# A hybrid decoder step on one NeuronCore: a tile of its own for retrieved values, and transposes of repeated keys one step later

## The chip, the cores and the metric

The kernel runs on one core of one Trainium2 chip. The time is the device time of one execution in microseconds (us), and the median of several executions is compared. The engines of the core are TensorE (PE, matrix multiplication, with PEld for the loading of its stationary operand), VectorE (DVE), ScalarE (ACT), GpSimd (POOL) and SyncE (SP, which here only issues transfers). Each engine works through its own instructions in order; semaphores hold it until what it needs is there.

## What is computed

One step of a decoder layer for 256 prompt tokens and 8 × 8 sample tokens, 320 columns in all. `trunk` runs a SwiGLU block, a token mixer and a second SwiGLU block. The mixer's one input projection feeds an mLSTM branch with 4 heads of 256 × 256 state and a dilated attention branch with 8 heads; sigmoid gates merge the two. The sample tokens start from a given state `C0`, `n0` of each of 8 sequences and read a cache of 2048 keys and values. The part of the reference that the change touches is the mLSTM of one chunk:

```python
num = jnp.einsum('bhts,bshv->bthv', wgt, v) \
    + jnp.transpose(sc, (0, 2, 1))[..., None] * jnp.einsum('bthk,bhkv->bthv', q, C0)
den = jnp.sum(wgt, axis=-1) + sc * jnp.einsum('bthk,bhk->bht', q, n0)
h = num / jnp.transpose(jnp.maximum(jnp.abs(den), jnp.exp(-m)), (0, 2, 1))[..., None]
...
C_new = sT[..., None, None] * C0 + jnp.einsum('bhs,bshk,bshv->bhkv', e, k, v)
n_new = sT[..., None] * n0 + jnp.einsum('bhs,bshk->bhk', e, k)
```

For the sample tokens, `q · C0` is what the kernel calls retrieval, and `C_new` is the state update, for 8 sequences × 4 heads.

## The kernel before, in words

**The weight stream.** All weights are float32 and come through one stream. A job is 256 output columns; a chunk is four k-tiles of 128 × 256 of a job (512 KB). SP loads a chunk into one of 5 `raw` buffers, ACT casts it to the upper part `hi` (L225) and DVE subtracts for the lower part `lo` (L226), each with 3 buffers. PE then makes three matmuls for every 128 × 128 block (`hi` by the upper part of x, `hi` by its lower part, `lo` by the upper), 24 for a chunk, into a PSUM tile `fg`. These are the instructions called `fg` in the profile, written by the helper at L144.

**Everything else** is written as Python generators, and `run_job` (from L272) sets the order: before the matmuls of chunk `ci` it splits chunk `ci + 2` if that isn't done, runs one step of the generators in `even` or in `odd` alternately, by a pace of 8 in 15 one step of `slow`, and one of each in `every`, then issues loads ahead up to chunk `ci + 7`. So what a step issues stands in each engine's queue between the work of two chunks. `mlstm` (L979) is in `odd`, one step every two chunks, 48 `fg` matmuls apart; the attention of the sample tokens is in `slow`. The small matmuls and transposes (L337) of these go to `bg`, a PSUM tag with 4 slots.

**SP** issues all transfers in the order written. A load into a tile waits, on SP, until the tile that had its slot is no longer in use, and a transfer waits for the one issued eight before.

**The tile pool `m2`** (`m2_tile`, L500): 9 slots of 128 × 512 that go round in order of allocation. Each request takes the slot whose last holder is oldest, and the first instruction that writes the new tile waits until the last reader of the old one is done, be it an engine or a transfer. The states `C` (two for each pair of sequences, loaded by `load_c`, updated in place at L1135 and written back to `out_C_sample`), `vq`, `z`, `krep`, `vs`, `kw`, `kr`, `cn` and `isb` all live there.

**One head of the mLSTM**, step by step. `prep(h)`: decay terms `z` (DVE, ACT), `krep`, the sample keys repeated for 4 sequences (POOL, L1046), and `vs`, a cast of the sample values (ACT, L1057). `front(h)`: q · k products, transposes of `k` to `ka` and of `krep` to `kb` on PE, then on ACT `kw` from `ka` (L1089) and `kr` from `kb` (L1090). `update(h)`: PE multiplies `vh` by `kw` into the new prompt state, ACT copies it to `cn` (L1102), and POOL and ACT make `qm` (L1022) and the first `ks` (L1031 to L1033) from `kr`; then the next two states are loaded (`load_cc`). Then eight steps, two for each `s4`: `retrieve` multiplies `qm` by the states on PE, and in the last, `s4 == 3`, ACT copies the result to `isb` (L1126); `state` multiplies `ks` by `vs` and DVE adds the product to `C`; `make_ks` and `make_qm` prepare the next. `numer(h)` reads `isb`, and in the same step `prep(h + 1)` follows.

**The softmax of the sample attention** keeps small rows in `sm`, [128, 9, 32], of which each helper row is written once.

Of the kernel before, what the change touches and what calls it, by code (L numbers as in the profile page):

```python
# [9 lines left out]
F32 = mybir.dt.float32  # L10
F32R = mybir.dt.float32r
AF = mybir.ActivationFunctionType
OP = mybir.AluOpType
AX = mybir.AxisListType
# [114 lines left out]
def decoder_kernel(tc, I, O, K):  # L129
    nc = tc.nc  # L130
    V, S, G, T = nc.vector, nc.scalar, nc.gpsimd, nc.tensor
# [14 lines left out]
    def bcast(ap, n, at=1):  # L146
        shape = list(ap.shape)
        shape.insert(at, n)
        idx = [slice(None)] * len(ap.shape)
        idx.insert(at, None)  # L150
        return ap[tuple(idx)].to_broadcast(shape)
# [6 lines left out]
    def later(fn, n=1):  # L158
        later_q.append([n, fn])
# [94 lines left out]
    def bg_tile():  # L254
        return pp.tile([128, 512], F32, tag="bg", bufs=4, name="bg")
# [79 lines left out]
    def tr(out, in_):  # L335
        k = in_.shape[0]
        T.transpose(out, in_, ident[:k, :k])  # L337
# [156 lines left out]
    def mxt(shape, tag, bufs, name, dt=F32):  # L494
        return M["p"].tile(shape, dt, tag=tag, bufs=bufs, name=name)
# [4 lines left out]
    def m2_tile(name):  # L500
        return mxt([128, 512], "m2", 9, name)
# [113 lines left out]
    def sample_attention():  # L615
# [1 line left out]
        bdm = M["mix"][:, M_BD:M_BD + 32]  # L617
        kd = mxt([128, 10, 512], "kd", 1, "kd")
        pts = mxt([128, 3, 152], "pts", 1, "pts")
        sm = mxt([128, 9, 32], "sm", 1, "sm")  # L620
        G.memset(pts, 0.0)
        G.memset(sm, 0.0)
        G.memset(sm[:, 5], 1.0)
        kraw = {}

        def load_k(u, pr):
# [78 lines left out]
        def soft(u, sp):  # L705
            hg, b = divmod(u, 8)
            s = mxt([128, SCOLS], "s", 1, "ss")
            tb = ttab[:, hg]
            V.tensor_tensor(s[:, 0:128].rearrange("p (y c) -> p y c", c=4), sp[:, 0:128].rearrange("p (c y) -> p y c", c=4),
                            tb[:, 0:128].rearrange("p (y c) -> p y c", c=4), op=OP.add)  # L710
            V.tensor_tensor(s[:, 128:320].rearrange("p (x a r) -> p x a r", x=4, a=6),
                            sp[:, 128:320].rearrange("p (a x r) -> p x a r", x=4, a=6),
                            tb[:, 128:320].rearrange("p (x a r) -> p x a r", x=4, a=6), op=OP.add)
            V.tensor_tensor(s[:, 320:328], sp[:, 320:328], tb[:, 320:328], op=OP.add)
            V.tensor_reduce(sm[:, 0, 0:1], s, op=OP.max, axis=AX.X)
            V.transpose(sm[:, 1], sm[:, 0])
            V.tensor_reduce(sm[:, 2, 0:8], sm[:, 1].rearrange("p (i t) -> p t i", i=4), op=OP.max, axis=AX.X)
            V.tensor_scalar(sm[:, 3].rearrange("p (i t) -> p i t", i=4), bcast(sm[:, 2, 0:8], 4), -1.0, None, op0=OP.mult)
            V.transpose(sm[:, 4], sm[:, 3])
            S.activation(s, s, AF.Exp, bias=sm[:, 4, 0:1], accum_out=sm[:, 5, 0:1])  # L720
            return s

        def keys(u, p0, p1):
# [23 lines left out]
        def probs(s):  # L747
            pt = bg_tile()
            tr(pt[:, 0:128], s[:, 0:128])
            tr(pt[0:104, 128:256], s[:, 128:232])  # L750
            tr(pt[0:104, 256:384], s[:, 224:328])
            S.copy(pts[:, 0, 0:128], pt[:, 0:128])
            S.copy(pts[0:104, 1:3, 0:128], pt[0:104, 128:384].rearrange("p (c n) -> p c n", c=2))
            V.transpose(sm[:, 6], sm[:, 5])
            V.tensor_reduce(sm[:, 7, 0:8], sm[:, 6].rearrange("p (i t) -> p t i", i=4), op=OP.add, axis=AX.X)
            V.reciprocal(sm[:, 7, 0:8], sm[:, 7, 0:8])
            V.transpose(sm[:, 8], sm[:, 7])

        qbd = make_qbd(0)
        for u in range(17):  # L760
            yield
            if u:
                ob = bg_tile()
                pv(u - 1, ob)
            if u < 16:
                sp = scores(u, qbd)
            if u:
                if u % 4 == 1:
                    o4 = mxt([128, 4, 128], "o", 1, "osb")
                S.activation(o4[:, (u - 1) % 4], ob[:, 0:128], AF.Copy, scale=sm[:, 8, 0:1])  # L770
                if u % 4 == 0:
                    spawn(combine((u - 1) // 8, (u // 4 - 1) % 2, o4), even, True)
            if u == 16:
                break
            s = soft(u, sp)
            values(u, 4, 0, 2)
            keys(u + 1, 0, 1)
            yield
            if u < 15:
                qbd = make_qbd(u + 1)  # L780
            keys(u + 1, 1, 3)
            values(u, 1, 3, 5)
            yield
            probs(s)
            keys(u + 1, 3, 4)
            if u == 6:
                q4 = make_q4(1)
            yield
            keys(u + 1, 4, 5)
            yield  # L790
# [188 lines left out]
    def mlstm():  # L979
# [6 lines left out]
        aeT, sTb, nP, nS = M["aeT"], M["sTb"], M["nP"], M["nS"]  # L986
# [4 lines left out]
        H = {}  # L991
# [72 lines left out]

        def front(h):
            d = H[h]
            q, k, z, kp, vq, vs_ = (d[x] for x in ("q", "k", "z", "kp", "vq", "vs"))
            sp = bg_tile()
            for kt in range(2):
                mm(sp[:, 0:256], k[:, kt, 0:128], q[:, kt, 0:256], kt == 0, kt == 1)  # L1070
            for kt in range(2):
                mm(sp[:, 256:384], k[:, kt, 128:256], q[:, kt, 128:256], kt == 0, kt == 1)
            for kt in range(2):
                mm(sp[:, 384:448], k[:, kt, 192:320], q[:, kt, 256:320], kt == 0, kt == 1)
            ka, kb = bg_tile(), bg_tile()
            for j in range(2):
                for kt in range(2):
                    tr(ka[:, j * 256 + kt * 128:j * 256 + (kt + 1) * 128], k[:, kt, j * 128:(j + 1) * 128])
            for g in range(2):
                for kt in range(2):  # L1080
                    tr(kb[:, g * 256 + kt * 128:g * 256 + (kt + 1) * 128],
                       kp[:, kt * 256 + g * 128:kt * 256 + (g + 1) * 128])
            V.tensor_tensor(z[:, 0:448], z[:, 0:448], sp[:, 0:448], op=OP.mult)
            for x in (32, 96):
                V.tensor_tensor(vs_[x:x + 32], vq[x:x + 32], vs_[x:x + 32].bitcast(F32), op=OP.subtract)
            kw = m2_tile("kw").rearrange("p (j c) -> p j c", j=2)
            kr = m2_tile("kr")
            for j in range(2):
                S.activation(kw[:, j], ka[:, j * 256:(j + 1) * 256], AF.Copy, scale=aeT[:, j, 4 + h:5 + h])  # L1089
            S.copy(kr, kb)  # L1090
            d.update(kw=kw, kr=kr)

        def update(h):
            d = H[h]
            kw, ke, v = (d[x] for x in ("kw", "ke", "v"))
            cu = [bg_tile(), bg_tile()]
            for kt in range(2):
                for j in range(2):
                    mm(cu[kt][:, 0:257], kw[:, j, kt * 128:(kt + 1) * 128], v[:, j], j == 0, j == 1)
            cn = m2_tile("cn")  # L1100
            for kt in range(2):
                S.copy(cn[:, kt * 256:(kt + 1) * 256], cu[kt][:, 0:256])  # L1102
                V.tensor_copy(nP[:, 2 * h + kt:2 * h + kt + 1], cu[kt][:, 256:257])
            nk = mxt([128, 2, 8], "nk", 1, "nk")
            V.tensor_reduce(nk, ke.rearrange("p k (b t) -> p k b t", b=8), op=OP.add, axis=AX.X)
            for kt in range(2):
                V.tensor_tensor(nSv[:, :, h, kt], n0v[:, :, h, kt], sTv[:, h], op=OP.mult)
                V.tensor_tensor(nSv[:, :, h, kt], nSv[:, :, h, kt], nk[:, kt], op=OP.add)
            make_qm(h, 0)
            make_ks(h, 0)  # L1110
            later(lambda: dma(O["C_prompt"][0, 0, h].rearrange("(k p) v -> p k v", p=128),
                              cn.rearrange("p (k v) -> p k v", k=2)), 2)

        def retrieve(h, s4):
            d = H[h]
            if s4 == 0:
                d["ip"] = bg_tile()
            ip, qm = d["ip"], d["qm"]
            for kt in range(2):
                for n in range(2):  # L1120
                    x = 32 * (kt * 2 + n)
                    mm(ip[x:x + 32, 0:256], qm[:, kt, n], Cq[0][n][:, kt * 256:(kt + 1) * 256], s4 == 0, s4 == 3,
                       tile_position=(0, x))
            if s4 == 3:
                d["isb"] = m2_tile("isb")[:, 0:256]
                S.copy(d["isb"], ip[:, 0:256])  # L1126

        def state(h, b):
# [533 lines left out]
    sp = token_sums([(Y["sq"], 1)])  # L1662
# [57 lines left out]
```

## Time and profile before

| | |
|---|---|
| median of 3 runs | 2978.39 us (2976.34 to 2979.70) |
| the profiled execution | 2980.88 us |
| its span | 2979.1 us |
| mean granted PE clock | 0.992 |
| PE busy | 2923.1 us, 98% of the span |
| DVE busy | 1638.5 us, 55% |
| ACT busy | 1086.4 us, 36% |
| POOL busy | 233.8 us, 8% |
| HBM traffic | 186 GB/s over the span, up to 310 in a fortieth of it |

In a timeline the number on the left of a row is the time from the start of the span. The mixer runs from about 1060 to 1790 us, its four mLSTM heads between 1260 and 1750 us. In rows of a timeline, the bracket says how long the engine had been idle and which instruction or transfer ended the wait. A wait for several things at once is put down to the one that came last in the profile, so the name can be that of a neighbour.

### The profile page before, as it was taken

How to read it: one execution, taken by the hardware profiler on the slowest of the kernel's cores; microseconds unless marked ns; L12 is line 12 of the kernel's file. 1: busy time of each engine (PE TensorE's matmuls, PEld its weight loads, DVE VectorE, ACT ScalarE, POOL GpSimd, SP SyncE). 2: the span in 40 equal slices, each digit the busy share in tenths (PEclk: the TensorE clock that was granted, in tenths of full speed). 3: DMA queues.
4: the chain of work that ended last, by engine and by line, in shares of the span. 5: the costliest groups of instructions: out<-in, count | busy, mean ns of one | idle time of the engine just before them, and what ended most of it. 6: DMA issues, size and time to landing. Idle time of an engine off the chain costs nothing.

```text
span 2979.1 us, 51248 instructions
## 1 busy us (share of the span) xinstructions
PE 2923.1 (98%) x21522; PEld 2877.3 (97%) x21522; DVE 1638.5 (55%) x1863; ACT 1086.4 (36%) x1364; POOL 233.8 (8%) x258
## 2 busy tenths in 40 slices
PE   9999999999999999988989999999999999999998
PEld 9999999999999999987988999999999999999998
DVE  6444444444446656876877876655444444444444
ACT  5332333333335333333443433334333332333334
POOL 0000000000000000122322210000000000000000
PEclk9999999999999999999999999999999999999999
DMA  6445454444546679898989987554444444445443
GB/s 209 147 147 169 143 154 149 149 146 152 156 142 188 202 214 296 257 282 250 303 249 310 288 264 252 183 177 153 149 153 151 149 146 152 150 141 161 150 140 108
DMA packets 507763, 557.22 MB, mean 187 GB/s; under 512 B 30156, under 2 KB 452604, under 8 KB 507508
## 3 DMA queue, kind: packets, MB, share of 16 engines
q1 hardware_dynamic: 506828, 552.43, 61.0%
q8 instruction: 168, 2.75, 0.4%
q10 hardware_dynamic: 704, 1.52, 0.1%
q14 instruction: 63, 0.52, 0.1%
HBM read 521.58 MB, written 32.28 MB: 186 GB/s over the span
## 4 chain that ended last, share of the span: by engine, by line
PE 51%; issue 2%; DVE 1%; POOL 0%; DMA 0%; SPq 0%; ACT 0%; POOLq 0%; DVEq 0%
PE fg L144 48%; PE bg L144 3%; PE bg L337 0%; DVE sg L970 0%; SPq L141 0%; DVE lo L226 0%; DMA vt<-in_cache_v_dram 0%; DVE pre L940 0%; POOLq L1716 0%; DMA kraw<-in_cache_k_dram 0%; POOL Y L1680 0%; POOL ks L1033 0%; DVE C L1135 0%; DVE kd L639 0%; ACT xn L1431 0%
## 5 line engine op out<-in xcount | busy, mean ns | idle before, releaser
L226 DVE TENSOR_TENSOR lo<-raw,hi 128x1024 fp32r<-128x1024 f32 (+1 forms) x780 | 961.0, 1234 | 973.5 <-ACT hi L225 955.1
L144 PE MATMUL fg<-xh,hi 128*128 128x320 f32 x4240 | 1320.2, 312 | 0.5 <-ACT hi L1515 0.3
L144 PE MATMUL fg<-xh,lo 128*128 128x320 f32 x4240 | 1310.5, 310 | 1.8 <-DVE lo L226 1.8
L144 PE MATMUL fg<-xl,hi 128*128 128x320 f32 x4240 | 1310.2, 310 | 0.0
L225 ACT CAST hi<-raw 128x1024 fp32r<-128x1024 f32 (+1 forms) x780 | 801.8, 1030 | 1162.6 <-PE fg L144 1016.7
L144 PEld LDWEIGHTS fg<-xh,hi 128*128 128x128 f32 x4240 | 798.1, 189 | 2.7 <-ACT hi L1515 0.7
L144 PEld LDWEIGHTS fg<-xh,lo 128*128 128x128 f32 x4240 | 797.7, 188 | 2.8 <-DVE lo L226 2.5
L144 PEld LDWEIGHTS fg<-xl,hi 128*128 128x128 f32 x4240 | 798.3, 189 | 0.8
L144 PE MATMUL fg<-hh,hi 128*128 128x320 f32 x1408 | 437.7, 311 | 0.0
L144 PE MATMUL fg<-hh,lo 128*128 128x320 f32 x1408 | 435.1, 309 | 0.0
L144 PE MATMUL fg<-hl,hi 128*128 128x320 f32 x1408 | 435.0, 309 | 0.0
L144 PEld LDWEIGHTS fg<-hh,hi 128*128 128x128 f32 x1408 | 264.3, 188 | 1.7 <-issue 1.6
L144 PEld LDWEIGHTS fg<-hl,hi 128*128 128x128 f32 x1408 | 264.3, 188 | 1.0 <-issue 1.0
L144 PEld LDWEIGHTS fg<-hh,lo 128*128 128x128 f32 x1408 | 264.3, 188 | 0.0
L448 POOL TENSOR_TENSOR gt<-gt,rstd 128x640 f32<-128x640 f32 x44 | 69.5, 1579 | 1865.2 <-ACT gt L447 1838.7
L144 PE MATMUL fg<-bh,hi 128*128 128x320 f32 x512 | 158.4, 309 | 0.0
L144 PE MATMUL fg<-bl,hi 128*128 128x320 f32 x512 | 158.2, 309 | 0.0
L144 PE MATMUL fg<-bh,lo 128*128 128x320 f32 x512 | 158.2, 309 | 0.0
L639 DVE STREAM_TRANSPOSE kd<-kraw 128x1024 f32<-128x1024 f32 x80 | 96.4, 1219 | 15.0 <-DMA kraw<-in_cache_k_dram 14.7
L144 PEld LDWEIGHTS fg<-bh,hi 128*128 128x128 f32 x512 | 96.1, 188 | 0.2 <-issue 0.2
L144 PEld LDWEIGHTS fg<-bl,hi 128*128 128x128 f32 x512 | 96.1, 188 | 0.0
L144 PEld LDWEIGHTS fg<-bh,lo 128*128 128x128 f32 x512 | 96.1, 188 | 0.0
(297 smaller groups left out, 1510.4 us busy)
## 6 DMA issues: line engine op xcount, KB each, us to landing
raw<-in_w_in_dram SPq DMA_DIRECT2D x176, 512.0 KB
raw<-in_w_ffb_in_dram SPq DMA_DIRECT2D x176, 512.0 KB
raw<-in_w_ffa_in_dram SPq DMA_DIRECT2D x175, 512.0 KB
raw<-in_w_ffa_out_dram SPq DMA_DIRECT2D x80, 512.0 KB
raw<-in_w_ffb_out_dram SPq DMA_DIRECT2D x80, 512.0 KB
kraw<-in_cache_k_dram SPq DMA_DIRECT2D x96, 256.0 KB
vt<-in_cache_v_dram SPq DMA_DIRECT2D x128, 192.0 KB
kraw<-in_cache_k_dram SPq DMA_DIRECT2D x32, 512.0 KB
```

The source lines that it names most:

```text
L144: T.matmul(out, a, b, start=start, stop=stop, **kw)
L225: S.copy(hi[:, :nk], t[:, :nk])
L226: V.tensor_tensor(lo[:, :nk], t[:, :nk], hi[:, :nk].bitcast(F32), op=OP.subtract)
L448: G.tensor_tensor(gt, gt, bcast(rstd, 2), op=OP.mult)
L639: V.transpose(kd[:, 2 * pr:2 * pr + 2].rearrange("p a b -> p (a b)"), t.rearrange("p a b -> p (a b)"))
```

## The change

Three edits, all in the mixer. The result of the retrieval, `isb`, gets a tile of its own with one buffer; it was the first half of an `m2` slot. The transposes of `krep` and the copy `kr` move from `front(h)` into `update(h)`, one mLSTM step later. The softmax's `sm` has 7 rows instead of 9: rows 1 and 5 are used twice, all on DVE. The number of instructions on each engine stays as it is.

```diff
-            ka, kb = bg_tile(), bg_tile()
+            ka = bg_tile()
...
-            for g in range(2):
-                for kt in range(2):
-                    tr(kb[:, g * 256 + kt * 128:g * 256 + (kt + 1) * 128],
-                       kp[:, kt * 256 + g * 128:kt * 256 + (g + 1) * 128])
...
             kw = m2_tile("kw").rearrange("p (j c) -> p j c", j=2)
-            kr = m2_tile("kr")
             for j in range(2):
                 S.activation(kw[:, j], ka[:, j * 256:(j + 1) * 256], AF.Copy, scale=aeT[:, j, 4 + h:5 + h])
-            S.copy(kr, kb)
-            d.update(kw=kw, kr=kr)
+            d.update(kw=kw)

         def update(h):
             d = H[h]
-            kw, ke, v = (d[x] for x in ("kw", "ke", "v"))
+            kw, ke, v, kp = (d[x] for x in ("kw", "ke", "v", "kp"))
+            kb = bg_tile()
+            for g in range(2):
+                for kt in range(2):
+                    tr(kb[:, g * 256 + kt * 128:g * 256 + (kt + 1) * 128],
+                       kp[:, kt * 256 + g * 128:kt * 256 + (g + 1) * 128])
+            kr = m2_tile("kr")
+            S.copy(kr, kb)
+            d["kr"] = kr
             cu = [bg_tile(), bg_tile()]
...
             if s4 == 3:
-                d["isb"] = m2_tile("isb")[:, 0:256]
+                d["isb"] = mxt([128, 256], "isb", 1, "isb")
                 S.copy(d["isb"], ip[:, 0:256])
...
-        sm = mxt([128, 9, 32], "sm", 1, "sm")
+        sm = mxt([128, 7, 32], "sm", 1, "sm")
```

On PE, in `front(0)` and `update(0)`, the transposes of `krep` leave the place behind those of `k` (`ident` is the identity matrix by which PE transposes):

```order
 L144 MATMUL bg<-q,k 128x64 x2
 L337 MATMUL bg<-ident,k 128x128 x4
-L337 MATMUL bg<-ident,krep 128x128 x4
 L144 MATMUL fg<-xh,hi 128x320
 L144 MATMUL fg<-xl,hi 128x320
@@ -8239,4 +8238,5 @@
 L144 MATMUL fg<-xl,hi 128x320
 L144 MATMUL fg<-xh,lo 128x320
+L337 MATMUL bg<-ident,krep 128x128 x4
 L144 MATMUL bg<-vh,kw 128x257 x4
```

The four transposes stand 48 `fg` matmuls later, ahead of the product for the prompt state, and so in each head.

On ACT, in `front(1)` and `update(1)`, the copy `kr` follows (`re` at the table loads is the norm of head 0's output):

```order
-L1169 ACTIVATE re<-hh 128x640
-L1089 ACTIVATE kw<-bg,aeT 128x256 x2
-L1090 COPY kr<-bg 128x512
-L225 CAST hi<-raw 128x1024 x2
-L1178 ACT_TABLE_LOAD
-L1178 ACTIVATE re<-bg,epst 128x320
-L1179 ACT_TABLE_LOAD
-L1179 ACTIVATE re<-re 128x320
-L1102 COPY cn<-bg 128x256 x2
```

That is the order before, and this is the one after:

```order
+L1171 ACTIVATE re<-hh 128x640
+L1084 ACTIVATE kw<-bg,aeT 128x256 x2
+L225 CAST hi<-raw 128x1024 x2
+L1180 ACT_TABLE_LOAD
+L1180 ACTIVATE re<-bg,epst 128x320
+L1181 ACT_TABLE_LOAD
+L1181 ACTIVATE re<-re 128x320
+L1096 COPY kr<-bg 128x512
+L1104 COPY cn<-bg 128x256 x2
```

The copy now stands behind two casts of weights and the norm, directly ahead of `cn` and `ks`.

On ACT, at the last retrieval of head 0, the order stays and the semaphores for which `isb` waits change (those named DMAHW are of transfers):

```order
 L225 CAST hi<-raw 128x1024 [waits DMAHW5_49,PE_49,Activation_49]
-L1126 COPY isb<-bg 128x256 [waits DMAHW5_49,DMAHW6_49,DVE_49,PE_49]
+L1128 COPY isb<-bg 128x256 [waits PE_49]
 L1031 ACTIVATE ks<-kr,eb 128x256
 L1032 ACTIVATE kf<-kr,eb 64x256 [waits Pool_49]
 L930 ACTIVATE y<-pre,gv 128x256
```

`isb` waits for PE alone after the change. The `m2` slots that it took now go to the tiles that are allocated behind it: the slot of head h's last such C tile to the `vs` of head h + 1.

More of the change, by code (lines that the diff above doesn't have):

```diff
@@ L619, in sample_attention @@
         pts = mxt([128, 3, 152], "pts", 1, "pts")
-        sm = mxt([128, 9, 32], "sm", 1, "sm")
+        sm = mxt([128, 7, 32], "sm", 1, "sm")
         G.memset(pts, 0.0)
         G.memset(sm, 0.0)
-        G.memset(sm[:, 5], 1.0)
+        G.memset(sm[:, 4], 1.0)
         kraw = {}
@@ L717, in soft @@
             V.tensor_reduce(sm[:, 2, 0:8], sm[:, 1].rearrange("p (i t) -> p t i", i=4), op=OP.max, axis=AX.X)
-            V.tensor_scalar(sm[:, 3].rearrange("p (i t) -> p i t", i=4), bcast(sm[:, 2, 0:8], 4), -1.0, None, op0=OP.mult)
-            V.transpose(sm[:, 4], sm[:, 3])
-            S.activation(s, s, AF.Exp, bias=sm[:, 4, 0:1], accum_out=sm[:, 5, 0:1])
+            V.tensor_scalar(sm[:, 1].rearrange("p (i t) -> p i t", i=4), bcast(sm[:, 2, 0:8], 4), -1.0, None, op0=OP.mult)
+            V.transpose(sm[:, 3], sm[:, 1])
+            S.activation(s, s, AF.Exp, bias=sm[:, 3, 0:1], accum_out=sm[:, 4, 0:1])
             return s
@@ L753, in probs @@
             S.copy(pts[0:104, 1:3, 0:128], pt[0:104, 128:384].rearrange("p (c n) -> p c n", c=2))
+            V.transpose(sm[:, 1], sm[:, 4])
+            V.tensor_reduce(sm[:, 5, 0:8], sm[:, 1].rearrange("p (i t) -> p t i", i=4), op=OP.add, axis=AX.X)
+            V.reciprocal(sm[:, 5, 0:8], sm[:, 5, 0:8])
             V.transpose(sm[:, 6], sm[:, 5])
-            V.tensor_reduce(sm[:, 7, 0:8], sm[:, 6].rearrange("p (i t) -> p t i", i=4), op=OP.add, axis=AX.X)
-            V.reciprocal(sm[:, 7, 0:8], sm[:, 7, 0:8])
-            V.transpose(sm[:, 8], sm[:, 7])
         qbd = make_qbd(0)
@@ L769, in sample_attention @@
                     o4 = mxt([128, 4, 128], "o", 1, "osb")
-                S.activation(o4[:, (u - 1) % 4], ob[:, 0:128], AF.Copy, scale=sm[:, 8, 0:1])
+                S.activation(o4[:, (u - 1) % 4], ob[:, 0:128], AF.Copy, scale=sm[:, 6, 0:1])
                 if u % 4 == 0:
@@ L1066, in front @@
             d = H[h]
-            q, k, z, kp, vq, vs_ = (d[x] for x in ("q", "k", "z", "kp", "vq", "vs"))
+            q, k, z, vq, vs_ = (d[x] for x in ("q", "k", "z", "vq", "vs"))
             sp = bg_tile()
@@ L1078, in front, with update @@
                     tr(ka[:, j * 256 + kt * 128:j * 256 + (kt + 1) * 128], k[:, kt, j * 128:(j + 1) * 128])
+            V.tensor_tensor(z[:, 0:448], z[:, 0:448], sp[:, 0:448], op=OP.mult)
+            for x in (32, 96):
+                V.tensor_tensor(vs_[x:x + 32], vq[x:x + 32], vs_[x:x + 32].bitcast(F32), op=OP.subtract)
+            kw = m2_tile("kw").rearrange("p (j c) -> p j c", j=2)
+            for j in range(2):
+                S.activation(kw[:, j], ka[:, j * 256:(j + 1) * 256], AF.Copy, scale=aeT[:, j, 4 + h:5 + h])
+            d.update(kw=kw)
+        def update(h):
+            d = H[h]
+            kw, ke, v, kp = (d[x] for x in ("kw", "ke", "v", "kp"))
+            kb = bg_tile()
             for g in range(2):
@@ L1082, in front @@
                        kp[:, kt * 256 + g * 128:kt * 256 + (g + 1) * 128])
[L1083 to L1086, printed above, removed]
             kr = m2_tile("kr")
-            for j in range(2):
-                S.activation(kw[:, j], ka[:, j * 256:(j + 1) * 256], AF.Copy, scale=aeT[:, j, 4 + h:5 + h])
             S.copy(kr, kb)
-            d.update(kw=kw, kr=kr)
-        def update(h):
-            d = H[h]
-            kw, ke, v = (d[x] for x in ("kw", "ke", "v"))
+            d["kr"] = kr
             cu = [bg_tile(), bg_tile()]
```

## The prediction

> **What bounds the kernel now.** I read the page first: which engine is busy, and how much of the span it is not.
>
> ```profile
> PE 2923.1 (98%) x21522; PEld 2877.3 (97%) x21522; DVE 1638.5 (55%) x1863; ACT 1086.4 (36%) x1364; POOL 233.8 (8%) x258
> ```
>
> PE works 2923.1 of 2979.1 us, so no edit that leaves its 18,713 instructions as they are can win more than the other 56 us, plus what PE runs at a lower clock. The second view is the list of waits, for PE and then for ACT, between 1250 and 1760 us, where the four mLSTM heads run. Its columns are us in total, times, longest.
>
> ```profile
> PE bg L144 <- POOL ks L1033: 25.1, 4, 14.3
> PE bg L337 <- POOL krep L1046: 5.6, 1, 5.6
> PE bg L337 <- issue: 5.1, 1, 5.1
> PE bg L144 <- POOL qm L1022: 2.3, 1, 2.3
> PE fg L144 <- DVE lo L226: 1.1, 1, 1.1
> ...
> ACT isb L1126 <- DMA kraw<-in_cache_k_dram: 19.1, 1, 19.1
> ACT isb L1126 <- DMA out_C_sample_dram<-C: 12.2, 1, 12.2
> ACT isb L1126 <- issue: 8.0, 1, 8.0
> ```
>
> 39 of PE's 56 idle us stand in five lines, and the first three are what the change touches. The wait for `ks` looks like POOL's fault and is not: ACT makes `ks` only after `isb`, and `isb` waited three times on a transfer. The timelines show one of them, in head 0 (start, duration, what; in brackets the idle time before it and what ended it):
>
> ```profile
> 1379.39 0.37 ACT L1126 COPY isb<-bg 128x256 f32<-128x256 f32 x1 [19.10 <-DMA kraw<-in_cache_k_dram]
> 1380.20 0.50 ACT L1032 ACTIVATE kf<-kr,eb 64x256 f32<-64x256 f32 x1
> 1381.56 1.03 ACT L225 CAST hi<-raw 128x1024 fp32r<-128x1024 f32 x1
> 1381.61 0.79 PE L144 MATMUL bg<-vs,ks 128*128 128x256 f32 x2 [14.26 <-POOL ks L1033]
> ```
>
> ACT stands before `isb` for 19.10 us, then `kf` and POOL's `ks` follow and PE's state matmul starts 2.2 us after `isb`, having lost 14.26 us. The cast of the next weights is queued behind `isb` too. The releaser named is the load of keys that ended nearest; what `isb` needs is its `m2` slot, which a C tile held whose write-back was under way. The other two cases have the same form (12.2 and 8.0 us on ACT).
>
> The third view is the table of stretches (us; busy us of PE, PEld, DVE, ACT, POOL; granted clock, DMA share, GB/s).
>
> ```profile
> 1300.00:1320.00 20.00, 18.51 (x131) 17.64 (x129) 17.84 (x27) 9.40 (x17) 5.69 (x5) 1.00 1.02 316
> 1320.00:1340.00 20.00, 19.22 (x225) 16.97 (x226) 18.60 (x17) 6.78 (x10) 5.44 (x8) 0.91 0.91 260
> ...
> 1360.00:1380.00 20.00, 7.35 (x50) 7.08 (x49) 3.04 (x3) 0.90 (x3) 0.00 (x0) 0.80 0.87 250
> 1380.00:1400.00 20.00, 18.39 (x216) 17.04 (x217) 18.50 (x25) 8.01 (x13) 8.76 (x16) 0.86 0.79 230
> 1400.00:1420.00 20.00, 20.00 (x136) 19.46 (x136) 17.80 (x31) 12.96 (x20) 5.34 (x4) 1.00 0.72 227
> 1420.00:1440.00 20.00, 18.72 (x128) 17.34 (x127) 19.79 (x27) 9.24 (x17) 6.65 (x7) 1.00 0.99 306
> ```
>
> A stall costs more than its length: after the stall the clock is 0.86 in 1380 to 1400. If the missing 0.14 is time at half clock, that is 5.6 us, of which PE idled 1.6 and worked 4.0, which loses 2.0 us. And once PE has stalled for 14 us DVE has none to spare: it is busy 17.8 to 19.8 of 20 us in the three stretches from 1380 on.
>
> **The change part by part.** Taken naively it frees 24.9 us of `ks` (14.26, and 3.67 and 7.01 below), 10.7 of `krep`, and five times 2.0 us of half clock: 45 us. Each place has something that is late next.
>
> *The scratch rows of the softmax* (`sm` 9 to 7) rename operands on DVE, with the same instructions and no new wait on another engine: 0.
>
> *Head 0, `krep`.* PE's transposes of `krep` move behind 48 weight matmuls, so this wait goes.
>
> ```profile
> 1274.82 1.25 DVE L639 STREAM_TRANSPOSE kd<-kraw 128x1024 f32<-128x1024 f32 x1 [11.55 <-DMA kraw<-in_cache_k_dram]
> 1277.02 1.22 DVE L226 TENSOR_TENSOR lo<-raw,hi 128x1024 fp32r<-128x1024 f32 x1
> 1279.40 1.24 PE L337 MATMUL bg<-ident,krep 128*128 128x128 f32 x4 [5.63 <-POOL krep L1046]
> ```
>
> But DVE was itself held to 1274.82 by a load of keys, and the `lo` that the next weight matmuls read is done at 1278.2. PE starts 1.2 us earlier, and the next wait, 2.3 us for `qm`, takes that up: it ends with a run of DVE that has hardly a gap (17.84 of 20 us, 1300 to 1320). I take 0; at most it is 5.6 + 2.0.
>
> *Head 0, `isb`.* With its own tile `isb` waits for PE alone and ACT goes on. Two limits come next, the transfers and DVE:
>
> ```profile
> 1381.36 1.86 DVE L932 SCALAR_TENSOR_TENSOR y<-pre,gv,y 128x256 f32<-128x256 f32 x6 [17.99 <-ACT y L930]
> 1395.65 1.21 DVE L226 TENSOR_TENSOR lo<-raw,hi 128x1024 fp32r<-128x1024 f32 x1
> ...
> 1374.73 7.71 SPq L141 DMA_DIRECT2D q<-qs_d  x8
> 1382.54 0.53 SPq L141 DMA_DIRECT2D raw<-in_w_in_dram  x1
> ...
> GB/s 261 208 216 245 287 323 351 375 313 221 149 100 190 357 332 256 293 227 197 106 60 39 0 62 220 344 78 165 369 136 253 250 261 231 300 309 382 374 375 387
> ```
>
> The last line is what the DMA engines moved in each us from 1360 on. DVE could start its chain up to 18 us earlier, but SP issues the raw weights behind eight `q` fills, at 1382.54, and 62 + 220 + 344 GB/s in 1383 to 1386 are 626 KB, so the 524 KB of that chunk are there at about 1386.5, no sooner without the stall, for SP waited for no engine here. A cast of 1.03 us, and its `lo` starts at 1387.8 instead of 1395.65: 7.9 us earlier. From there DVE's chain is the pace, so PE wins 7.9 less some 0.4 of new small waits: 7.5 us, and the clock's 2.0 are within it. Were the transfer no limit it would be 14.3 + 2.0 = 16.3; were DVE not to use its start at all, 0.
>
> *Heads 1 and 2, `isb`.*
>
> ```profile
> 1497.28 0.50 PE L144 MATMUL bg<-vs,ks 128*128 128x256 f32 x2 [3.67 <-POOL ks L1033]
> ...
> 1616.05 1.04 ACT L225 CAST hi<-raw 128x1024 fp32r<-128x1024 f32 x1
> 1616.93 0.80 PE L144 MATMUL bg<-vs,ks 128*128 128x256 f32 x2 [7.01 <-POOL ks L1033]
> 1617.12 1.23 DVE L226 TENSOR_TENSOR lo<-raw,hi 128x1024 fp32r<-128x1024 f32 x1 [8.78 <-ACT hi L225]
> ```
>
> Head 2 is the clean case: ACT's cast and DVE's `lo` were themselves held by `isb`, so both come early with PE. It wins 7.01 and, of the clock, up to 2.0; I take 8.4. Head 1 would win 3.67 and a part of the 2.0, 5.2 in all, if it kept them.
>
> *Head 2, `krep`.* The second transposes' wait ends with no releaser named:
>
> ```profile
> 1524.73 1.08 PE L337 MATMUL bg<-ident,krep 128*128 128x128 f32 x4 [5.08 <-issue]
> 1524.25 0.38 ACT L753 COPY pts<-bg 104x256 f32<-104x256 f32 x1
> 1528.24 0.56 ACT L1090 COPY kr<-bg 128x512 f32<-128x512 f32 x1
> 1537.07 0.74 ACT L966 ACTIVATE sg<-sg 128x640 f32<-128x640 f32 x1 [4.81 <-DVE sg L400]
> 1543.97 0.74 POOL L1033 TENSOR_TENSOR ks<-kf,ks 64x256 fp32r<-64x256 f32 x1 [3.51 <-ACT kf L1032]
> 1545.04 0.50 PE L144 MATMUL bg<-vs,ks 128*128 128x256 f32 x2
> ```
>
> It starts 0.1 us after ACT has copied `pts` out of a PSUM tile, so it waited for one of the four `bg` slots. Whoever allocates next, the convolution's transposes, will stand before the same slot. And head 2's first state matmul (1545.04) is only 0.3 us behind its `ks` (1543.97 + 0.74), which hangs on ACT's `sg` and through it on DVE. This chain moves up by head 1's 5.2 us and not by the 5.08 of `krep`, and the moved `kr` copy now lies in it, 0.56 us. So heads 1 and 2 together win between 3.6 and 5.2 up to here; I take 4.2. If the slot were free at once, another 5.1 + 2.0.
>
> *The moved copy* of `kr` adds 0.56 us to ACT ahead of `cn` and `ks` in each `update`. In the other heads ACT's 36% leave room for it; at worst it is 3 × 0.56 = 1.7 us.
>
> *The moved wait.* The C tile whose slot `isb` took is now followed in it by head h+1's `vs` cast (ACT, L1057), one step later. ACT holds it in order, with the weight casts behind it, so PE would feel it as it does now. Head 1's `vs`:
>
> ```profile
> 1402.81 0.60 ACT L1057 CAST vs<-vq 128x512 fp32r<-128x512 f32 x1
> ```
>
> The write-back that released `isb` had landed by 1379.39, and `vs` comes at 1402.81 − 7.9, 15.5 us behind: 0.
>
> Sum: 0 + 7.5 + 8.4 + 4.2 = 20.1 us less. The profiled execution took 2980.88 us for its span of 2979.1; it would be 2960.8. It lies 2.5 us above the median of the three runs, 2978.39, so the median to expect is 2978.4 − 20.1 = **2958.3 us**.
>
> The Trainium skill, "TensorE: Matmul & The Clock Gate", section "Part 1: The HAM clock gate", states that the array drops to half clock after at least one idle window of about 3.4 us, and that the window is free-running. The 0.86 above agrees, but here the clock also dropped behind the 2.3 us wait for `qm` (0.91 in 1320 to 1340, in the table), so a short wait is not safe; by the page's 3.4 us the small waits that I leave behind would cost no clock, and the sum would be some 2 us larger.
>
> **The rivals.**
>
> *Most of the stalls' time is won (about 36 us, 2942 us).* If the raw weights of head 0 come earlier, because SP's queue moves up too, head 0 gives up to 16.3, and if the PSUM slot is free, 7.1 more in head 2. For it: DMA shares of 0.72 to 0.87 in 1360 to 1420 leave room. Against it: the eight `q` fills took SP 7.71 us, whatever PE did. Chance 0.14.
>
> *DVE or the transfers take most of it back (about 10 us, 2968 us).* DMA shares of 0.99 to 1.02 and a DVE at 17.8 to 19.8 of 20 us stand in the table; if the queue of loads is the pace of the whole mLSTM stretch, only head 2's `isb` and a remnant stay. Against it: PE has just 1.1 us of waits for `lo` now. Chance 0.19.
>
> *The wait only changes its place (0, 2978 us).* `vs` or the loads behind it then stand before the same write-backs as long as `isb` did. It needs landings over 15 us later than now. Chance 0.07.
>
> *Slower: SP stands before the C load.* The first load of C after `update` takes the slot of `krep`, so it now waits for transposes that PE does one step (48 matmuls, each 20 / 136 = 0.147 us by the row of 1400 to 1420: 7.1 us) later, and all raw weights queue on SP behind it.
>
> ```profile
> 1416.42 1.90 PE L144 MATMUL bg<-vh,kw 128*128 128x257 f32 x8
> 1423.11 0.96 SPq L141 DMA_DIRECT2D C<-in_state_C_dram  x2
> ```
>
> SP gets there 6.7 us after PE's `update` of head 1, so it doesn't wait. It decides as soon as SP runs ahead of PE by more than the weights' slack; a full step in each of four heads is 28 us, less the 20 won: 8 us slower, 2986 us. Chance 0.05.
>
> **How the numbers follow.** My case has 0.55, the others 0.14, 0.19, 0.07 and 0.05. About 0.2%, 6 us, is what a measurement of this kernel can tell from no change. Faster by more than that: 0.55 + 0.14 + nearly all of 0.19 = 0.87; same 0.08; slower 0.05. My case's own bounds are 3.6 + 7.0 + 5.5 − 1.7 = 14.4 us (no clock won at either `isb`, the copies paid) and 5.2 + 9.0 + 9.9 = 24.1 us (all of it won), that is 2954 to 2964. The range reaches on over the second rival and to the middle of the first: 2943 to 2970.
>
> **What would show it.** Right: the lines of `isb` on ACT and of `krep` on PE are gone, the `ks` lines shrink from 25.1 to under 5 us, a few new waits for `hi`, `lo` or a PSUM slot of 10 to 15 us in all stand in their place, and PE idles about 40 instead of 56 us. Head 0 moves PE up by 7 to 8 us by 1430, head 2 by another 8 behind its last `isb`. Wrong: a `vs` line on ACT or a C load on SP that waits long, head 0 gaining over 12 or under 4 us, or a PE idle time that stays near 56.

## The result and the profile after

The changed kernel took 2957.82 us (median of 4 runs, 2957.03 to 2960.00), the kernel before 2977.98 us (4 runs, 2976.34 to 2979.70): 20.2 us less, a ratio of 0.9933 with a 95% interval of 0.9916 to 0.9951. The prediction was 2958.3 us.

The page of the changed kernel, span 2955.7 us, has the same busy time on PE, to 2 us:

```profile
PE 2921.1 (99%) x21522; PEld 2873.5 (97%) x21522; DVE 1638.3 (55%) x1863; ACT 1085.5 (37%) x1364; POOL 233.5 (8%) x258
```

So 2955.7 − 2921.1 = 34.6 us of idle time are left of 56 (I had said about 40), and nearly all of the gain is idle time that went. The list of PE's waits between 1250 and 1760 us (total, times, longest) says which:

```profile
PE fg L144 <- DVE lo L226: 7.3, 4, 4.3
PE bg L337 <- ACT re L1180: 4.2, 2, 4.0
PE bg L144 <- POOL qm L1022: 3.7, 3, 2.5
PE fg L144 <- ACT hi L225: 1.3, 2, 1.0
PE bg L337 <- ACT pts L753: 0.5, 1, 0.5
PE bg L144 <- POOL ks L1033: 0.2, 1, 0.2
```

The three lines that the change aimed at fell from 35.8 us to 0.2, and the list as a whole from 39.2 to 17.2: 14 us of new waits stand where 36 went. What a line of waits names is not what an edit wins.

Where along the span it was won is read from one instruction that both traces have in the same order, the first state matmul of each head (PE, `bg<-vs,ks`):

| start, us | before | changed | step |
|---|---|---|---|
| head 0, next to last | 1359.81 | 1359.69 | −0.1 |
| head 1, first | 1427.02 | 1416.70 | −10.2 |
| head 2, first | 1545.04 | 1530.80 | −3.9 |
| head 3, first | 1661.32 | 1637.89 | −9.2 |
| end of the span | 2979.1 | 2955.7 | 0.0 |

Head 0's `isb`, ACT in the changed kernel (start, duration, idle time before):

```profile
1360.08 0.36 ACT L1128 COPY isb<-bg 128x256 f32<-128x256 f32 x1
1360.35 0.51 ACT L1031 ACTIVATE ks<-kr,eb 128x256 fp32r<-128x256 f32 x1
...
1375.18 1.04 ACT L225 CAST hi<-raw 128x1024 fp32r<-128x1024 f32 x1 [7.00 <-DMA raw<-in_w_in_dram]
...
1384.28 1.05 ACT L225 CAST hi<-raw 128x1024 fp32r<-128x1024 f32 x1 [7.22 <-DMA raw<-in_w_in_dram]
...
1392.53 0.61 ACT L1057 CAST vs<-vq 128x512 fp32r<-128x512 f32 x1
```

`isb` follows the cast ahead of it without a wait. ACT now waits for what was hidden behind it, twice 7 us for raw weights. And `vs`, which took over the slot of the C tile, waits for nothing.

DVE and SP at the same place:

```profile
1376.26 1.23 DVE L226 TENSOR_TENSOR lo<-raw,hi 128x1024 fp32r<-128x1024 f32 x1 [4.10 <-ACT hi L225]
...
1385.36 1.23 DVE L226 TENSOR_TENSOR lo<-raw,hi 128x1024 fp32r<-128x1024 f32 x1 [2.22 <-ACT hi L225]
...
1373.65 5.98 SPq L141 DMA_DIRECT2D q<-qs_d  x8
1379.74 0.53 SPq L141 DMA_DIRECT2D raw<-in_w_in_dram  x1
```

The raw weights behind the eight fills are issued at 1379.74 (1382.54 before), and their `lo` starts at 1385.36 (1395.65 before): 10.3 us earlier, and head 1's first state is 10.3 us earlier. The stretches, PE busy first, then granted clock, DMA share and GB/s at the end:

```profile
1360.00:1380.00 20.00, 20.00 (x208) 19.78 (x210) 14.51 (x19) 7.02 (x12) 3.33 (x7) 1.00 0.77 225
1380.00:1400.00 20.00, 17.79 (x159) 16.05 (x152) 16.36 (x32) 7.22 (x14) 5.01 (x12) 0.98 0.85 255
1400.00:1420.00 20.00, 18.44 (x111) 16.25 (x110) 18.95 (x24) 13.18 (x21) 9.04 (x8) 0.93 1.07 288
```

PE is busy 20.00 us where it was 7.35, at the full clock; 2.2 of these 12.7 us are given back in the two rows behind it, where PE waits 3.8 us in all, most of it for `hi`, `lo` and `qm`.

### The profile page after: what moved, and what is told of

It is laid out like the page before. It is cut to its first block, busy times and chain, and to the rows that moved or that the text cites. A ratio compares the mean times of both kernels' runs of the same rounds, so it can differ in the third digit from the quotient of the medians.

```text
span 2955.7 us, 51237 instructions
## 1 busy us (share of the span) xinstructions
PE 2921.1 (99%) x21522; PEld 2873.5 (97%) x21522; DVE 1638.3 (55%) x1863; ACT 1085.5 (37%) x1364; POOL 233.5 (8%) x258
## 4 chain that ended last, share of the span: by engine, by line
PE 92%; DMA 4%; DVE 2%; ACT 1%; issue 0%; SPq 0%; POOL 0%; POOLq 0%; DVEq 0%; ACTq 0%
PE fg L144 87%; PE bg L144 4%; PE bg L337 1%; DMA vt<-in_cache_v_dram 1%; DMA raw<-in_w_in_dram 1%; DMA kraw<-in_cache_k_dram 1%; DVE lo L226 1%; DVE pre L940 0%; DMA vh<-vm_d 0%; DMA vm_d<-stage 0%; DMA vq<-vm_d 0%; DVE sg L970 0%; ACT hi L225 0%; DMA xl<-in_x_prompt_dram 0%; DMA out_v_prompt_dram<-stage 0%
```

## The experiments

Each was timed beside the kernel before on the same chip; the medians of before in the series were 2978.61, 2978.46 and 2978.55 us.

**One edit alone: the tile of `isb`.** The changed kernel with the transposes of `krep` and the copy `kr` back in `front`. With nine rows of `sm` the mixer's pool would need 124.31 KB per partition of the 124.09 that are left, so the smaller `sm` belongs to this edit:

```diff
         def front(h):
...
-            ka = bg_tile()
+            ka, kb = bg_tile(), bg_tile()
...
+            S.copy(kr, kb)
+            d.update(kw=kw, kr=kr)

         def update(h):
...
-            kr = m2_tile("kr")
-            S.copy(kr, kb)
-            d["kr"] = kr
```

> Only the tile of its own for isb (with the seven rows of the softmax); the transposes of krep stay in front. My theory, by which the move of krep wins nothing of its own: 20 us less than before (18 to 23), PE's waits for ks gone, its waits for krep still there in heads 0 and 2, 4 to 6 us each. Rival, by which each edit is worth the waits that its lines name: 25 us of ks and its half clock go but the 10.7 us of krep and their clock stay, and as the change as a whole won 20, this wins 8 to 13.

Measured: 2958.65 us (2953.26 to 2961.45, 5 runs), 0.9932 (0.9919 to 0.9944), 20 us less. The tile alone gives what the change as a whole gives. Its waits of PE:

```profile
PE bg L337 <- POOL krep L1046: 5.7, 1, 5.7
PE bg L337 <- DVE ss L714: 4.2, 1, 4.2
PE bg L337 <- issue: 4.0, 1, 4.0
```

`krep` keeps its waits, and one shows up in head 1 that isn't in the list of before (4.2 us, for a PSUM slot that DVE's softmax held). So my theory's total holds. Head 1's first state stands only 5.3 us ahead of before here, and 10.3 us in the changed kernel, but that difference is a transfer's. SP and DVE in head 0:

```profile
1383.94 1.32 SPq L141 DMA_DIRECT2D raw<-in_w_in_dram  x1
...
1390.36 1.23 DVE L226 TENSOR_TENSOR lo<-raw,hi 128x1024 fp32r<-128x1024 f32 x1 [3.31 <-ACT hi L225]
```

The raw weights behind the fills are issued 4.2 us later than in the changed kernel (1379.74), their `lo` starts 5.0 us later (1385.36 there), and head 1's first state stands as much behind (1421.71 against 1416.70). The wait of 4.2 us lies inside this lateness of DVE. The medians (2958.65 here; 2957.82 and 2955.78 for the changed kernel) don't tell the move apart from nothing.

**The other edit alone: `krep`.** The changed kernel with `isb` in its pool slot:

```diff
-                d["isb"] = mxt([128, 256], "isb", 1, "isb")
+                d["isb"] = m2_tile("isb")[:, 0:256]
```

> Only the move of the transposes of krep and of the copy kr; isb stays in its slot of the pool. My theory: within 3 us of before; krep's two waits of 5.6 and 5.1 us turn into waits for lo in head 0 and for a PSUM slot (convolution transposes) in head 2, and the three waits for ks stay, the one of head 2 as long as before. Rival: the waits of krep are won, 8 to 12 us less than before.

Measured: 2979.51 us (2974.45 to 2986.90, 11 runs), 1.0002 (0.9993 to 1.0010): nothing. Its profiled execution was its slowest (2986.90), so only the kind of its waits is read, not their size:

```profile
PE bg L144 <- POOL ks L1033: 28.4, 4, 15.0
PE fg L144 <- DVE lo L226: 8.1, 3, 6.3
PE bg L337 <- ACT re L1180: 2.6, 2, 2.5
```

The waits for `krep` are gone and about the same time is waited for `lo` in head 0 and for the norm's PSUM tile in head 2. The rival's 8 to 12 us are refuted.

**Copy `isb` later instead.** Before, with the copy taken out of `retrieve` and written behind `make_ks`:

```diff
-            if s4 == 3:
-                d["isb"] = m2_tile("isb")[:, 0:256]
-                S.copy(d["isb"], ip[:, 0:256])
...
+        def keep_isb(h):
+            d = H[h]
+            d["isb"] = m2_tile("isb")[:, 0:256]
+            S.copy(d["isb"], d["ip"][:, 0:256])
...
                 make_ks(h, s4 + 4)
+                if s4 == 3:
+                    keep_isb(h)
```

> Before, with isb still in its slot of the pool, but its copy written behind ks and kf on ACT, so that it no longer holds them. My theory, by which ACT's order carries the wait to the weight casts and to DVE as well: PE's waits for ks go, but in head 0 PE runs into weights that aren't cast, and DVE's chain starts at 1381 as before, so head 0 wins 0 to 3 us, head 1 about 4, head 2 about 7 to 9: 10 to 14 us less than before. Rival, by which the wait of PE for ks is the whole of the cost: as much as with the tile of its own, 18 to 23 us less.

Measured: 2958.47 us (2956.60 to 2961.51, 5 runs), 0.9933 (0.9921 to 0.9946): 20 us less, the rival's number. But the trace shows that this wasn't the experiment I meant:

```profile
1360.75 0.51 ACT L1032 ACTIVATE kf<-kr,eb 64x256 f32<-64x256 f32 x1
1361.29 0.38 ACT L1128 COPY isb<-bg 128x256 f32<-128x256 f32 x1
```

`isb` doesn't wait at all. The instruction's semaphores are now PE's and ACT's own, no transfer's: the pool gave it another slot, that of `kr`, whose last reader is the `kf` just ahead. That is so in heads 0 and 2; in head 1 it got the slot of the other C tile of the pair, whose write-back stands further ahead in SP's queue, and there too it doesn't wait. The slots don't simply go round, as I wrote above; as the built program has them, a request gets the slot whose holder is done first in the program, and at the old place `kr` was still to be read. A move of one copy gives the gain of the change without a byte of memory.

**The same, with the slot held.** On top of that, `kr` and `vs` are read once more a step later, so that `isb` is given the same C tile's slot as before in every head, and stands before the same write-backs:

```diff
+            d["ks"], d["kf"] = ks, kf
...
+        def late_reads(h):
+            d = H[h]
+            S.copy(d["kf"][0:32, 0:1], d["kr"][0:32, 0:1])
+            S.copy(d["kf"][0:32, 0:1], d["vs"][0:32, 0:1].bitcast(F32))
...
                 state(h, s4 + 4)
+                if s4 == 3:
+                    late_reads(h)
```

> Before, with the copy of isb behind ks and kf on ACT, and with kr and vs read once more in the next step (two copies of 32 x 1 on ACT in each head that nothing uses), so that isb is given the slot of the same C tile as before and waits for the same write-back. My theory, by which ACT's order carries that wait to the casts and to DVE: ACT stands 18 us before isb in head 0 as before, PE's wait for ks goes, but waits for hi or lo come in its place, and head 0 wins 0 to 3 us; with about 4 in head 1 and 7 in head 2 it is 9 to 14 us less than before. Rival, by which the wait for ks is the whole of the cost: 18 to 23 us less, with ACT waiting as long.

Measured: 2973.49 us (2969.80 to 2980.45, 11 runs), 0.9985 (0.9976 to 0.9994): 5 us less. ACT and PE, waits:

```profile
PE fg L144 <- ACT hi L225: 11.5, 3, 8.3
PE bg L337 <- POOL krep L1046: 5.6, 1, 5.6
PE fg L144 <- DVE lo L226: 5.1, 5, 1.8
PE bg L337 <- issue: 5.1, 1, 5.1
...
ACT isb L1128 <- DMA out_C_sample_dram<-C: 15.9, 1, 15.9
```

With `ks` out of the way ACT still stands 15.9 us before `isb`, and PE now runs into weights that ACT hasn't cast (8.3 us once). Three quarters of the 20 us hang on the casts and DVE's chain behind `isb`, not on `ks`. That refutes the rival. My own 9 to 14 us were too many: by the four places of the table above its profile's steps are +1.4, −3.1, +0.1 and −3.3 us, so head 1 won nothing where I had put 4, with 2.8 us of new waits for `hi` and `lo`, and head 2 gives back 2.9 us for `hi`.

**Where `krep` waited without a name.** Before, with the convolution's transposes started six steps later:

```diff
     def conv_out():
-        yield
+        for _ in range(6):
+            yield
```

> Before, with the four convolution transposes started six steps later. My theory, by which krep's wait in head 2 is one for a PSUM slot: the wait of 5.1 us without a releaser is gone, but head 2's first ks is late next, so no more than 2 us are won. Rival 1, by which it is krep itself or ACT that is late: the wait stays at 5 us. Rival 2: wait and half clock are both won, 6 to 7 us less than before.

Measured: 2978.45 us (2975.79 to 2984.96, 11 runs), 1.0003 (0.9994 to 1.0012): nothing won. Its list has no wait of head 2's `krep`; in its place stand 1.4 us for `hi`, 0.7 for `lo` and this one for `ks`:

```profile
1541.56 0.80 PE L144 MATMUL bg<-vs,ks 128*128 128x256 f32 x2 [3.00 <-POOL ks L1034]
```

So the 5.1 us were a PSUM slot, and behind it `ks` is late by as much. One more thing is in this trace: head 0's stall, some 130 us ahead of the first instruction that differs, is 10.89 us instead of 14.26. A step of a single profile that ends with a transfer moves by 3 us from run to run.

**The changed kernel once more**, as a reference in its series.

> The changed kernel once more, beside the others of this series: 20 us less than before, and in its profile the same three steps (head 0 about 10, heads 1 and 2 about 4, head 2's last about 9). A second profile shows how far such a step moves from run to run; the waits of head 0, which hang on when transfers land, could move by 3 us.

Measured: 2955.78 us (2953.63 to 2958.19, 5 runs), 0.9928 (0.9915 to 0.9940). Its steps are −0.9, −11.1, −6.4 and −9.2 us, by the same four places as in the table. Head 2's differs most: the wait for the norm's tile was 3.0 instead of 4.0 us, and no half clock followed. Behind the first state of head 3, 2.5 us are given back until the end of the span (2954.0).

**The convolution's transposes later, in the changed kernel**, by the same edit.

> The changed kernel, with the four convolution transposes started six steps later. My theory, by which they wait in head 2 for the PSUM slot that krep waited for before, and head 2's ks is late next: their wait of 4.0 us goes, PE then waits for ks at head 2's first state or hardly at all, and 2 to 2.5 us are won over the changed kernel. Rival 1: wait and half clock are both won, 6 us. Rival 2: the slot is late for whoever comes, and nothing is won.

Measured: 2956.97 us (2955.35 to 2960.75, 5 runs), 0.9933 (0.9921 to 0.9946): no better than the changed kernel beside it. The 4.0 us are gone, and PE waits as long at head 2's first state for its `ks` (the releaser named is a neighbour), after which the clock is low:

```profile
1528.55 0.69 PE L144 MATMUL bg<-vs,ks 128*128 128x256 f32 x2 [3.86 <-DMA gate_d<-sg]
...
1520.00:1540.00 20.00, 15.49 (x200) 13.07 (x199) 13.40 (x26) 11.89 (x19) 4.01 (x5) 0.91 0.84 246
```

Head 2's first state is 2.3 us earlier than in the changed kernel's first profile, as my theory had it; by the fifth state 2.0 of these are lost again at the half clock that follows the wait. Of the sum, rival 2 was right.

**The fills of `q` further apart, in the changed kernel.**

```diff
-                later(lambda i=i: fill(i), (1, 1, 2, 3)[i])
+                later(lambda i=i: fill(i), (1, 2, 3, 4)[i])
```

> The changed kernel, with the four q fills (four transfers of 32 KB each) one chunk apart and no longer two of them together, so that fewer stand ahead of the raw weights of head 0. My theory, by which head 0's DVE chain starts when that chunk has landed: it lands 1 to 3 us earlier, and head 0 wins as much, 1 to 3 us less than the changed kernel. Rival, by which DVE's own work is the pace there: no difference within 1 us.

Measured: 2953.34 us (2950.13 to 2957.31, 5 runs), 0.9920 (0.9906 to 0.9933). SP and DVE:

```profile
1371.08 2.58 SPq L141 DMA_DIRECT2D q<-qs_d  x4
1373.82 0.48 SPq L141 DMA_DIRECT2D raw<-in_w_in_dram  x1
...
1380.87 1.23 DVE L226 TENSOR_TENSOR lo<-raw,hi 128x1024 fp32r<-128x1024 f32 x1
```

The raw weights are issued at 1373.82, and `lo` follows DVE's own work without a gap, 2.8 us earlier than in the changed kernel's second profile and 4.5 earlier than in its first. Head 1's first state moves by the same (1412.22 against 1415.00 and 1416.70). That shows the transfer as the limit of head 0 in the changed kernel, and DVE as the next one. The medians differ by 2.4 us, within their intervals.

**The loads of head 0 split, on top of that.** `vh` and the first two C tiles one step later:

```diff
         load_head(0)
+        yield
         load_vals(0)
         load_cc(0)
         yield
-        yield
         prep(0)
```

> The kernel with the q fills one chunk apart, and the loads of vh and of the first two C tiles (896 KB) one mLSTM step later, behind the loads of keys that DVE waits for in head 0. My theory, by which the gain of krep in head 0 is eaten by these keys: they land some 3 us earlier, PE's wait for lo at 1279 falls from 4.4 to 1 to 2 us, and 2 to 3 us are won over the kernel with the fills apart. Rival, by which the wait for qm in the same head takes it up: PE is earlier at 1285 and level again at 1322, nothing won.

Measured: 2954.60 us (2953.83 to 2957.49, 5 runs), 0.9922 (0.9908 to 0.9935): nothing over the kernel with the fills apart.

```profile
1274.17 0.41 PE L144 MATMUL fg<-xh,lo 128*128 128x320 f32 x1 [1.22 <-DVE lo L226]
1283.13 0.43 PE L144 MATMUL bg<-vt,pts 96*32 96x128 f32 x8 [3.15 <-DMA vt<-in_cache_v_dram]
```

The wait for `lo` fell from 4.4 to 1.2 us, as it should if the late keys held it, and 9 us on PE waits 3.15 us for values, another transfer. The rival was right that another wait takes it up, but it is not the one for `qm` that it named.

**The norm behind `update`, on top of the fills.**

```diff
-            rms_sum(h)
             if h < 3:
                 update(h + 1)
                 load_cc(4 * h + 5)
+            rms_sum(h)
```

> The kernel with the q fills one chunk apart, and the sum of squares of the norm behind update in the program, so that on ACT kr, cn and the first ks come before the norm's two table loads, and on PE the tile of the norm is the last that is allocated. My theory, by which head 2's stall (4.0 us and its half clock) is the norm's tile held by ACT, with ks 2.5 us behind it: the wait of the convolution transposes goes, the first ks of heads 1 to 3 come 3 us earlier, and 2 to 6 us are won. Rival: the convolution transposes wait as long for kr's tile, which ACT copies no earlier than sg lets it, and 0 to 1 us is won.

Measured: 2951.50 us (2950.62 to 2954.77, 4 runs), 0.9911 (0.9897 to 0.9924), 27 us less than before and the lowest median of all.

```profile
1515.81 0.58 ACT L1096 COPY kr<-bg 128x512 f32<-128x512 f32 x1
...
1516.44 0.66 PE L337 MATMUL bg<-ident,cvn 128*128 128x128 f32 x4 [1.14 <-ACT kr L1096]
...
1521.12 0.50 PE L144 MATMUL bg<-vs,ks 128*128 128x256 f32 x2
```

The transposes wait 1.14 us for `kr`'s tile instead of 4.0 for the norm's, and head 2's first state comes at 1521.12 instead of 1526.64, 5.5 us earlier, of which head 1 had 1.4. Against the kernel with the fills apart 1.8 us arrive in the median, within the interval: of the sum, neither my 2 to 6 us nor the rival's 0 to 1 is shown.

**All three together.**

> The q fills apart, the loads of head 0 split and the norm behind update in one kernel. If the three places are independent, the sum of the gains: 26 to 34 us less than before, 2945 to 2953 us. If the transfers are what is short in the whole mLSTM stretch, no better than the best of the two others.

Measured: 2954.69 us (2950.89 to 2959.88, 5 runs), 0.9921 (0.9908 to 0.9934): 24 us less than before, short of the 26 to 34 I gave for the sum, and no better than the best of the two others (2951.50) or the fills alone (2953.34). So the gains don't add up; that the transfers are the reason isn't shown. Its profiled execution was its slowest, with the 3 us for values in head 0 and 2.7 for `kr`'s tile. Whether the split loads cost something there, the intervals don't tell.

## Why the prediction was right, point by point

**The sum, 20.1 us predicted, 20.2 measured between medians.** Place by place the trace gives 23.4, because the profiled execution of before was slower than its median (2980.88 against 2977.98) and that of the changed kernel was not. So the terms below are compared with one another, and each is good to some 3 us. That the sum met the medians within 0.1 us is luck: my case's own bounds were 14.4 and 24.1 us. (The 18,713 instructions of PE stand in no row, the page counts 21,522; nothing is worked out from them.)

**Head 0, `krep`: 0 predicted, −0.1 measured.** The wait of 5.6 us turned into 4.3 us for `lo`, which DVE makes behind the load of keys that it waits for (`kd` at 1276.03, after 11.6 us), and 2.5 instead of 2.3 for `qm`. The move alone wins nothing. With the loads split the wait for `lo` fell from 4.4 to 1.2 us, so keys held it.

**Head 0, `isb`: 7.5 predicted, 10.2 and 11.1 in two profiles.** The mechanism held: the raw weights behind the fills, then DVE's chain. In all thirteen profiles, that of before among them, head 1's first state starts 31.3 to 31.7 us behind the start of that chunk's `lo`, so head 0 wins what this `lo` wins. The 2.7 us beyond the forecast come from the chunk, issued at 1379.74 and 1378.34 instead of 1382.54: SP had come to the eight fills 1.1 us earlier and took 5.98 instead of 7.71 us for them. That doesn't speak against "no sooner without the stall". With the fills as they were, the chunk was issued between 1379.70 and 1384.26 in the four profiles in which ACT stands before `isb`, and between 1378.34 and 1383.94 in the five in which it doesn't; the `lo` starts at 1395.0 and 1386.5 on average, 8.5 us earlier where I had 7.9. The forecast was nearer than the one pair of profiles makes it look, and a duration of a waiting queue is no constant.

**Head 2's last, `isb`: 8.4 predicted, 9.2 in both profiles.** The clean case was the one where all that would be late next was held by the same wait.

**Heads 1 and 2: 4.2 predicted together, 3.9 and 6.4.** The convolution's transposes did stand before a PSUM tile in `krep`'s place, 0.5 us for that of `pts` and 4.0 for the norm's. That the norm's tile, held through ACT's wait for `sg`, would be the longer I hadn't seen, though it is on the same chain that I read as the limit. `ks` itself then had 2.5 us to spare. In its trace the order of norm and `update` brought head 2's first state forward by 5.5 us, of which 2.7 are left at the end of the span; the medians don't show them.

**The clock: agreed in size.** In 1360 to 1400 it is 1.00 and 0.98 where it was 0.80 and 0.86. Read in half microseconds, the clock of before is 0.50 until about 1385.7, 4.1 us after PE starts again at 1381.61; that loses 2.0 us, as estimated. The half clock behind `qm` stayed in the first profile; in the second it did not come, after a wait of nearly the same length:

```profile
1320.00:1340.00 20.00, 19.41 (x226) 17.14 (x227) 18.57 (x18) 6.60 (x10) 5.25 (x8) 0.91 0.98 303
...
1320.00:1340.00 20.00, 19.26 (x231) 16.86 (x232) 18.72 (x20) 6.39 (x10) 4.25 (x7) 1.00 0.95 282
```

The first row is of the changed kernel's first profile (a wait of 2.5 us), the second of its repetition (2.3 us). In the first profile the clock is 0.50 from about 1320.8 to 1324.2 us, 3.4 us from the restart of PE on. The Trainium skill, "TensorE: Matmul & The Clock Gate", section "Part 1: The HAM clock gate", states a free-running window of about 3.4 us. The length of the drop agrees with it, but by the Trainium skill the clock drops after at least one idle window, and here PE had idled only 2.5 us. That it depends on where in the window a short wait falls would fit both profiles; no run tests it.

**The rivals.** Most of the stalls' time was not won: 14 us of new waits stand in the list. DVE and the transfers did take a part back, as the second rival feared, and ACT waits twice 7 us for raw weights in head 0, but 20 us were won and not 10. The wait did not move to `vs`. SP did not stand before the C load: in the changed kernel it gets there at 1415.51, 11.7 us behind the transposes of `krep` at 1403.79.

## What to carry to other kernels

When one engine casts weights and also empties other tiles, ask of each small copy which slot it is given and what is queued behind it: here a copy of 0.4 us held the weight stream, and either a tile of its own or a place behind `ks` and `kf`, where the pool has a slot that is done, frees 20 us. Price a stall by what is late next, not by its length: of 45 us that the waits and the clock named, 20 were won, and each edit beyond that met a new wait within two steps. A single profile places a gain; its size needs medians, since steps that end with a transfer move by 3 us and more from one execution to the next.

## What was not expected of the hardware

SP's time for the same eight transfers of 32 KB was 7.71, 5.98 and 7.02 us in three profiles, and the chunk behind them moved by up to 4.2 us with it (5.9 us over all profiles with these fills); head 0's stall was 14.26 and 10.89 us in two kernels that are the same up to there. The granted clock dropped to half behind the wait of 2.2 to 2.5 us for `qm` in head 0 in twelve of the thirteen profiles and not in one. What sets the one and the other was not tried.
